# Two decoder layers on one core: the opening's split moved ahead, the gate's modulation as PE bursts, rotary embedding in two operations, and the first layer's masks as PE products

## The chip, the core and the metric

The kernel runs on one core of one Trainium2 chip. The time is device microseconds of one execution on that core, and the median of the runs is compared. Engines: PE (TensorE, with PEld for its weight loads), DVE (VectorE), ACT (ScalarE), POOL (GpSimd); SP issues nearly all transfers.

## What is computed

Two layers (D = 1024, 256 tokens, one sequence, all float32). Each layer is a token mixer and a gated feed-forward part, both between norms whose scale, shift and gate come from a conditioning vector `c`. Cut to what the change touches:

```python
c_act = silu(c)
for l in range(2):
    sh_m, sc_m, gt_m, sh_f, sc_f, gt_f = split(c_act @ w_ada[l] + b_ada[l], 6)
    h = rms_norm(x, g_pre_mix[l]) * (1 + sc_m) + sh_m
    x = x + gt_m * rms_norm(token_mixer(h, ...), g_post_mix[l])
    h = rms_norm(x, g_pre_ffn[l]) * (1 + sc_f) + sh_f
    x = x + gt_f * rms_norm(conv_glu_ffn(h, ...), g_post_ffn[l])
# token_mixer: proj = h @ w_in -> mq mk mv dq dk dv (8 heads of 64 each), qi (8 heads), ki, wi
# rotary embedding on the first 16 of 64 dims of mq, mk, dq, dk, qi, ki
# mq mk mv: causal softmax attention (256 tokens are one block)
# indexer: score[t,s] = sum_h wi[t,h] relu(qi[t,h] . ki[s]); the 64 best admissible keys are kept
# dq dk dv: softmax attention over the kept keys; group norms; @ w_out
```

## The kernel before, in words

**Products in split precision.** A float32 weight tile is split into a high part (`wh`, made by ACT, L139) and a low part (`wl`, made by the DVE, L140); so are the activations (`hh`, `hl`). A product is three matmuls: hh.wh, hh.wl, hl.wh. All weights come in one stream in the order of use, by `load` (L108), into six rotating buffers of 1 MB (`raw`) that SP fills in order. A buffer is free when its split, or the reduction that reads it, is done.

**The opening** (`start`, L576) computes the first four chunks of the first layer's projection (ia, ib, mq, mk) while it computes the modulation of its input. It goes over eight blocks k of 128 features. For each, `modulation_v` (two reductions of 128x1024 on the DVE, L653) or, for k = 0, 3 and 6, `modulation` (eight matmuls of 32 columns by 256, L664, on the PE) gives shift and scale; `modulate` (L637) then splits the first 584 weight columns (`divide(k, 0)`), makes hh and f with two ACT operations (L644, L646), hl on the DVE (L647), and splits the other 1,024 columns (`divide(k, 1)`). `products` (L689) issues the 24 matmuls of a block. Everything here is pinned to the order of the program; block k + 1's modulation is written into the middle of block k's products.

**The mixer.** The PE's main line is `project` (L357) for mv, dq, dk, dv and then the output projection (`out_row`, 96 matmuls). Beside it run background chains (`Background`, L42): a chain is a generator that yields how many ticks it waits; the main line gives one tick for each k of a projection. Chains carry the gate and the feed-forward modulation (`gemv_v`, L182, one 128x1024 reduction a column on the DVE), the transposes of heads, the indexer (L393), the two attentions (`attend`, L427) and the group norms. `burst` (L384) issues a group of matmuls back to back. Between what is pinned a scheduler orders each engine's instructions by priority and by its own model of readiness.

**Scores and masks.** `scores` in `attend` computes a set of four heads by 128 keys, or two by 256, into banks 4 and 5, then one DVE operation a head (L449) adds the mask and takes the maximum into SBUF, ACT exponentiates that copy (L453), the DVE normalises (L461) and the PE transposes (L468). The masks are float32, 0 or -1e30: `lateneg` for the causal group, the indexer's two DVE operations (L423, L424) for the other.

**Embedding.** `rope_out` (L329) evacuates on ACT and applies the embedding with three DVE operations (L338 to L340). `ki_T` copies the transposed index key with the DVE (L757).

**The boundary** (L310) adds the gated, normed mixer output to x (`residual`, L290), normalises again, transposes and modulates; it needs the feed-forward scale and shift, so `bg.drain("sf")` stands before it (L859). The feed-forward part is 22 steps of `up` and `down`.

## Time and profile before

| | |
|---|---|
| median of 3 runs | 696.31 us (695.06 to 696.6) |
| the profiled execution | 694.81 us |
| its span in the trace | 693.0 us, mean granted clock 0.994 |
| PE / DVE / ACT busy | 662.4 / 560.6 / 422.4 us |
| moved by DMA | 163.02 MB, mean 235 GB/s |

The profile is of one execution; its span is from the first to the last instruction, and the execution's own time is 1.8 us longer. A matmul's end in the profile is modelled, so the distance from one start to the next tells more than its length. Busy time in a stretch of the trace is read against that stretch, not against the whole program: the stages have different limits.

### The profile page before, as it was taken

What the parts mean: (1) busy time and instruction counts of PE and PEld (TensorE: products, weight loads), DVE (VectorE), ACT (ScalarE), POOL (GpSimd) and SP (SyncE); (2) the same over time, 40 slices, a digit from 0 to 9 for tenths busy, and PEclk for the clock granted to TensorE, in tenths of its full rate; (3) what the DMA queues carried; (4) which work ended last, traced back from release to release, by engine and by line L of the source; (5) the groups of instructions that cost most, each with busy time, mean ns of one, the idle gap of its engine ahead of it and who ended that gap; (6) DMA issues with size and microseconds to landing.
All of it is one profiled execution on the core that took longest, in us unless ns stands there. A gap on an engine that the chain in (4) does not pass through costs nothing.

```text
span 693.0 us, 11206 instructions
## 1 busy us (share of the span) xinstructions
PE 662.4 (96%) x4257; PEld 569.1 (82%) x4257; DVE 560.6 (81%) x1130; ACT 422.4 (61%) x781; POOL 31.8 (5%) x56
## 2 busy tenths in 40 slices
PE   7999988997999999999999998999999999999996
PEld 4777766775899999999988776877789999999994
DVE  5779999999799999988669996678679886666553
ACT  5446567994865555555565657879586555555441
POOL 1000001012000000000020000000100000000000
PEclk9999999999999999999999999999999999999998
DMA  8997963766479999998444933345336895555001
GB/s 363 419 363 269 404 244 130 295 216 249 155 288 360 375 375 335 338 337 316 167 171 177 348 124 122 122 155 200 132 150 228 302 341 187 220 183 183 1 1 61
DMA packets 24517, 163.02 MB, mean 235 GB/s; under 512 B 3312, under 2 KB 3728, under 8 KB 6160
## 3 DMA queue, kind: packets, MB, share of 16 engines
q1 hardware_dynamic: 23184, 159.77, 61.2%
q0 software_dynamic: 704, 2.11, 1.0%
q8 instruction: 33, 0.54, 0.3%
q10 hardware_dynamic: 576, 0.43, 0.2%
q14 instruction: 20, 0.16, 0.1%
HBM read 161.24 MB, written 1.06 MB: 234 GB/s over the span
## 4 chain that ended last, share of the span: by engine, by line
PE 67%; DVE 18%; ACT 9%; issue 4%; POOL 1%; DMA 1%; SPq 0%; POOLq 0%; DVEq 0%; ACTq 0%
PE b L540 18%; PE b L539 18%; PE b L541 18%; PE b L369 7%; DVE raw L189 4%; DVE wl L140 3%; ACT t L453 2%; DVE iscore L420 2%; PE b L695 2%; DVE iscore L412 2%; DVE tiny L419 1%; PE b L389 1%; ACT wh L135 1%; ACT t L232 1%; PE b L468 1%
## 5 line engine op out<-in xcount | busy, mean ns | idle before, releaser
L140 DVE TENSOR_TENSOR wl<-raw,wh 128x1024 fp32r<-128x1024 f32 (+1 forms) x146 | 173.6, 1195 | 34.7 <-ACT wh L139 30.9
L539 PE MATMUL b<-hh,wh 128*128 128x256 f32 x640 | 180.0, 281 | 0.0
L541 PE MATMUL b<-hl,wh 128*128 128x256 f32 x640 | 179.7, 281 | 0.0
L540 PE MATMUL b<-hh,wl 128*128 128x256 f32 x640 | 179.7, 281 | 0.0
L139 ACT ACTIVATE wh<-raw 128x1024 fp32r<-128x1024 f32 (+1 forms) x146 | 149.2, 1045 | 45.2 <-PE b L541 36.4
L540 PEld LDWEIGHTS b<-hh,wl 128*128 128x128 f32 x640 | 122.5, 191 | 1.4
L539 PEld LDWEIGHTS b<-hh,wh 128*128 128x128 f32 x640 | 120.3, 188 | 1.4
L541 PEld LDWEIGHTS b<-hl,wh 128*128 128x128 f32 x640 | 120.1, 188 | 0.0
L189 DVE SCALAR_TENSOR_TENSOR raw<-raw,crow 128x1024 f32<-128x1024 f32 x80 | 96.2, 1219 | 1.4 <-DMA raw<-in_stream_dram 1.4
L369 PE MATMUL b<-wh,hh 128*128 128x512 f32 (+1 forms) x184 | 72.7, 397 | 0.0
L369 PE MATMUL b<-wh,hl 128*128 128x512 f32 (+1 forms) x184 | 68.5, 386 | 0.0
L139 ACT ACTIVATE dh<-raw 128x1024 fp32r<-128x1024 f32 (+2 forms) x47 | 49.7, 1059 | 25.8 <-PE b L540 25.8
L140 DVE TENSOR_TENSOR dl<-raw,dh 128x1024 fp32r<-128x1024 f32 (+2 forms) x47 | 56.8, 1210 | 8.9 <-ACT dh L139 8.9
L912 ACT ACTIVATE t<-b,smt 128x256 f32<-128x256 f32 x44 | 25.1, 571 | 57.4 <-PE b L541 57.3
L539 PE MATMUL b<-dh,t 128*128 128x512 f32 x152 | 59.7, 393 | 0.0
L540 PE MATMUL b<-dh,t 128*128 128x512 f32 x152 | 59.6, 392 | 0.0
L541 PE MATMUL b<-dl,t 128*128 128x512 f32 x152 | 59.2, 389 | 0.0
L369 PE MATMUL b<-wl,hh 128*128 128x512 f32 (+1 forms) x184 | 55.2, 391 | 2.7 <-DVE wl L140 2.7
L369 PEld LDWEIGHTS b<-wl,hh 128*128 128x128 f32 x184 | 33.9, 189 | 10.8 <-DVE wl L140 4.0
L369 PEld LDWEIGHTS b<-wh,hh 128*128 128x128 f32 x184 | 34.6, 188 | 7.3 <-issue 1.0
L369 PEld LDWEIGHTS b<-wh,hl 128*128 128x128 f32 x184 | 33.8, 188 | 5.9
L913 DVE SCALAR_TENSOR_TENSOR t<-b,smt,t 128x255 f32<-128x255 f32 x44 | 21.1, 480 | 20.7 <-ACT t L912 20.6
(167 smaller groups left out, 1105.2 us busy)
## 6 DMA issues: line engine op xcount, KB each, us to landing
raw<-in_stream_dram SPq DMA_DIRECT2D x143, 1024.0 KB, 6.5
raw<-in_stream_dram SPq DMA_DIRECT2D x8, 804.0 KB, 8.2
gate<-gated POOLq DMA_DIRECT2D x4, 512.0 KB, 7.0
xt<-in_x_dram SPq DMA_DIRECT2D x2, 512.0 KB, 4.1
raw<-in_stream_dram SPq DMA_DIRECT2D x1, 984.0 KB, 5.9
out_dram<-xt SPq DMA_DIRECT2D x2, 256.0 KB, 2.1
raw<-in_stream_dram SPq DMA_DIRECT2D x1, 328.0 KB, 5.0
out_dram<-xt ACTq DMA_DIRECT2D x1, 256.0 KB, 2.1
```

What stands on the lines that cost most here:

```text
L139: put(nc.scalar.activation(out=hi[:, :n], in_=raw, func=AF.Copy))
L140: put(nc.vector.tensor_tensor(out=lo[:, :n], in0=raw, in1=hi[:, :n].bitcast(F32), op=OP.subtract))
L189: nc.vector.scalar_tensor_tensor(out=ri, in0=ri, scalar=1.0, in1=crow, op0=OP.mult, op1=OP.mult, accum_out=mods[l][:, j + i:j + i + 1])
L369: mm = lambda l_, k, i, start=False, stop=False: nc.tensor.matmul(a[:, :n], lhsT=l_[:, k, tt], rhs=w[k][i], start=start, stop=stop)
L412: nc.vector.scalar_tensor_tensor(out=sc, in0=r[:, j * nk:j * nk + nk], scalar=wi[:, h:h + 1], in1=fill[:, 256 - nk:] if first else sc, op0 ...
L420: nc.vector.match_replace(out=sc, in_to_replace=m8, in_values=sc, imm_value=MARK)
L453: nc.scalar.activation(out=ev[:, j, :], in_=ev[:, j, :], func=AF.Exp, bias=nm[:, j:j + 1], scale=-1.0, accum_out=sm[:, j:j + 1])
L539: nc.tensor.matmul(y, lhsT=hh, rhs=wh, start=first, stop=False)
L540: nc.tensor.matmul(y, lhsT=hl, rhs=wh, start=False, stop=False)
L541: nc.tensor.matmul(y, lhsT=hh, rhs=wl, start=False, stop=last)
L912: nc.scalar.activation(out=z, in_=p[:, :256], func=AF.Identity, scale=w2[:, i:i + 1], bias=bc[:, i:i + 1])
L913: nc.vector.scalar_tensor_tensor(out=z[:, 1:], in0=p[:, :255], scalar=w1[:, i:i + 1], in1=z[:, 1:], op0=OP.mult, op1=OP.add)
```

## The change

Four parts. All lines below 192 are unchanged, so L139, L140 and L189 keep their numbers; later ones move by 22 and more.

1. In the opening `divide(k, 1)` comes before the two modulating ACT operations for k > 0.
2. The first layer's gate columns (16 to 24) go from eight DVE reductions to `gemv_p`: two rounds of two loads, a burst of 16 matmuls, an ACT copy, four transposes and one small DVE sum. The feed-forward shift columns (24 to 32) take the place of the gate in the early chain, with 6 ticks between, and only 32 to 40 are left to the later one.
3. `rope_out` multiplies by cosine and sine in one DVE operation over 16 columns twice, and adds the swapped half in a second; `ki_T` copies with ACT. Both layers.
4. In the first layer masks are bf16 zeros and ones. A product with `negi` (-1e30 times the identity) puts them into the score banks ahead of the scores, in the same burst; the DVE takes one maximum a bank, and ACT exponentiates from the bank.

```diff
+    def gemv_p(l, j0, j1, wait, gap):
+        yield wait
+        for j in range(j0, j1, 4):
+            r = [load(("p", l, j + 2 * i, 2048))[0] for i in range(2)]
+            yield gap
+            p = tp_bank()
+            burst([(p[32 * (i % 4):32 * (i % 4) + 32, 256 * h:256 * h + 256], cs32[:, i, :],
+                    r[h][:, 256 * i:256 * i + 256], dict(start=i < 4, stop=i >= 4, skip_group_check=True))
+                   for h in range(2) for i in range(8)])
+            e = t2()
+            nc.scalar.activation(out=e, in_=p, func=AF.Copy)
+            yield 4
+            q = tp_bank()
+            for b in range(4):
+                nc.tensor.transpose(q[:, 128 * b:128 * b + 128], e[:, 128 * b:128 * b + 128], ident)
+            nc.vector.tensor_reduce(out=mods[l][:, j:j + 4], axis=AX.X, op=OP.add,
+                                    in_=q.rearrange("p (b g r) -> p b g r", b=4, g=4)[:, :, :, 0])
+            yield 1
...
@@ rope_out
-        nc.vector.tensor_tensor(out=n[:, :, 0], in0=x, in1=cosv, op=OP.mult)
-        nc.vector.tensor_tensor(out=n[:, :, 1].rearrange("p h (a b) -> p h a b", a=2), in0=y, in1=sinv, op=OP.mult)
-        nc.vector.tensor_tensor(out=x, in0=n[:, :, 0], in1=n[:, :, 1], op=OP.add)
+        nc.vector.tensor_tensor(out=n, in0=x[:, :, None, :].to_broadcast([128, nh, 2, 16]),
+                                in1=rt[:, t][:, None].to_broadcast([128, nh, 2, 16]), op=OP.mult)
...
+        nc.vector.tensor_tensor(out=halves(x), in0=halves(n[:, :, 0]), in1=y, op=OP.add)
@@ indexer
+        if pe:
+            nc.vector.scalar_tensor_tensor(out=mask, in0=sc, scalar=-2.0e38, in1=late[:, 256 - nk:],
+                                           op0=OP.is_gt, op1=OP.max)
@@ attend, scores
+            left = masks[t] if masks is not None else lateb if pe else lateneg[:, 256 - nk:]
+            flags = dict(start=not pe, stop=True, skip_group_check=pe)
+            burst([(pv[:, :, nk - left.shape[-1]:], negi, left[:, None, :].to_broadcast([128, nh, left.shape[-1]]),
+                    dict(start=True, stop=False, skip_group_check=True)) for pv in (pp[::-1] if pe else ())]
+                  + [(pp[par][:, j, :], qT[64 * par:64 * par + 64, b * nh + j, 128 * t:128 * t + 128],
+                      kT[64 * par:64 * par + 64, b * nh + j, :nk], flags)
+                     for j in range(nh) for par in (1, 0)])
...
+                if pe:
+                    nc.vector.tensor_reduce(out=nm, in_=pv, axis=AX.X, op=OP.max, negate=True)
-                    nc.scalar.activation(out=ev[:, j, :], in_=ev[:, j, :], func=AF.Exp, bias=nm[:, j:j + 1],
-                                         scale=-1.0, accum_out=sm[:, j:j + 1])
+                    nc.scalar.activation(out=ev[:, j, :], in_=(pv if pe else ev)[:, j, :], func=AF.Exp,
+                                         bias=nm[:, j:j + 1], scale=1.0 if pe else -1.0,
+                                         accum_out=sm[:, j:j + 1])
@@ modulate, in the opening
             divide(k, 0)
+            if k:
+                divide(k, 1)
             xk = xT[k // 4][:, k % 4, :]
...
-            divide(k, 1)
+            if k == 0:
+                divide(k, 1)
@@ ki_T
-            nc.vector.tensor_copy(kiT[:, 128 * t:128 * t + 128], p[:, :128])
+            nc.scalar.copy(kiT[:, 128 * t:128 * t + 128], p[:, :128])
@@ the layers
-            bg.add("gt", gemv_v(l, 16, 24, 6))
+            bg.add("sf", gemv_v(l, 24, 32, 6))
+            bg.add("gt", gemv_p(l, 16, 24, 34, 16))
...
-            bg.add("sf", gemv_v(l, 24, 40, 9))
+            bg.add("sf", gemv_v(l, 32, 40, 9))
```

The order on the engines at three places, as the two programs have it. First the DVE in the opening, for k = 2: before, hl stands between the two low halves.

```order
L653 SCALAR_TENSOR_TENSOR raw,mod_99<-raw,crow 128x1024 x2
L639 SCALAR_TENSOR_TENSOR prescale<-mod_99,plus_161,smt 128x1
L641 TENSOR_TENSOR mod_99<-mod_99,smt 128x1
L140 TENSOR_TENSOR wl<-raw,wh 128x584
L647 TENSOR_TENSOR hl<-t_290,hh 128x256
L140 TENSOR_TENSOR wl<-raw,wh 128x1024
```

And in the changed program:

```order
L689 SCALAR_TENSOR_TENSOR raw,mod_99<-raw,crow 128x1024 x2
L672 SCALAR_TENSOR_TENSOR prescale<-mod_99,plus_161,smt 128x1
L674 TENSOR_TENSOR mod_99<-mod_99,smt 128x1
L140 TENSOR_TENSOR wl<-raw,wh 128x584
L140 TENSOR_TENSOR wl<-raw,wh 128x1024
L682 TENSOR_TENSOR hl<-t_294,hh 128x256
```

hl (L647, now L682) moved behind the wide low half; ACT's wide `wh` moved ahead of its two modulations in the same way.

Second, ACT at the end of the opening, before: the two splits of mv's first load come before the evacuations of ia (b_215, b_218), ib (b_214), mq (b_216, b_219) and mk (b_217, b_220).

```order
L139 ACTIVATE wh<-raw 128x1024 x3
L331 ACTIVATE t_592<-b_215 128x256
...
L331 ACTIVATE t_607<-b_214 128x256
L331 ACTIVATE t_635<-b_216 128x512
L331 ACTIVATE t_641<-b_219 128x512
L331 ACTIVATE t_647<-b_217 128x512
L331 ACTIVATE t_653<-b_220 128x512
L139 ACTIVATE wh<-raw 128x1024 x2
```

In the changed program:

```order
L353 ACTIVATE t_592<-b_215 128x256
...
L353 ACTIVATE t_605<-b_214 128x256
L139 ACTIVATE wh<-raw 128x1024 x2
L353 ACTIVATE t_629<-b_216 128x512
L353 ACTIVATE t_634<-b_219 128x512
L353 ACTIVATE t_639<-b_217 128x512
L353 ACTIVATE t_644<-b_220 128x512
L139 ACTIVATE wh<-raw 128x1024 x2
```

The four wide evacuations now stand between the first and the second pair of mv's splits.

Third, the DVE at the boundary, before: L189 are the reductions for scale and shift, L296 the residual's products, L304 its sums, L264 the normalising.

```order
L532 TENSOR_TENSOR o<-o,b_1623 128x512
L189 SCALAR_TENSOR_TENSOR raw,mod_99<-raw,crow 128x1024
L534 TENSOR_TENSOR hl<-o,hh 128x4x128
L189 SCALAR_TENSOR_TENSOR raw,mod_99<-raw,crow 128x1024 x3
L296 TENSOR_TENSOR t_1749<-b_1463,gate 128x512
L192 TENSOR_TENSOR mod_99<-mod_99,smt 128x16
L296 TENSOR_TENSOR t_1750<-b_1464,gate 128x512
L198 SCALAR_TENSOR_TENSOR prescale<-mod_99,smt 128x8
L304 SCALAR_TENSOR_TENSOR xt<-t_1749,tiny_1759,xt 128x512
L304 SCALAR_TENSOR_TENSOR xt<-t_1750,tiny_1759,xt 128x512
L296 TENSOR_TENSOR t_1773<-b_1465,gate 128x512
L264 TENSOR_SCALAR t_1778<-xt,tiny_1770 128x512
```

In the changed program, where these lines are L318, L326 and L286:

```order
L318 TENSOR_TENSOR t_1768<-b_1494,gate 128x512
L565 TENSOR_TENSOR o<-o,b_1654 128x512
L567 TENSOR_TENSOR hl<-o,hh 128x4x128
L318 TENSOR_TENSOR t_1769<-b_1495,gate 128x512
L326 SCALAR_TENSOR_TENSOR xt<-t_1768,tiny_1778,xt 128x512
L326 SCALAR_TENSOR_TENSOR xt<-t_1769,tiny_1778,xt 128x512
L189 SCALAR_TENSOR_TENSOR raw,mod_99<-raw,crow 128x1024
L140 TENSOR_TENSOR wl<-raw,wh 128x1024
L318 TENSOR_TENSOR t_1792<-b_1496,gate 128x512
L286 TENSOR_SCALAR t_1797<-xt,tiny_1789 128x512
```

No reduction stands ahead of the residual's first products any more; one, and a split, now stand between the sums and the normalising.

## Rows read from the trace of the kernel before

**Rows 1.** The page, part 1: busy time of each engine, its share of the span, and instructions.

```profile
PE 662.4 (96%) x4257; PEld 569.1 (82%) x4257; DVE 560.6 (81%) x1130; ACT 422.4 (61%) x781; POOL 31.8 (5%) x56
```

**Rows 2.** The table by stretches: start and end, its length, then for each engine busy us and instructions, the granted TensorE clock (1.00 is 2.4 GHz), the share of the DMA engines' time, GB/s. In order: the opening's eight blocks, the first layer's mixer up to its last output product, the boundary, the first layer's feed-forward part, the second layer's mixer.

```profile
12.30:57.80 45.50, 41.97 (x229) 32.08 (x230) 34.47 (x66) 25.55 (x46) 0.00 (x0) 1.00 0.99 390
57.80:163.40 105.60, 98.50 (x588) 75.32 (x586) 103.55 (x293) 75.72 (x165) 11.46 (x8) 1.00 0.69 261
163.40:176.40 13.00, 8.44 (x38) 6.54 (x38) 9.99 (x21) 7.95 (x23) 3.12 (x6) 0.87 0.44 163
181.00:350.00 169.00, 169.00 (x1209) 158.88 (x1208) 153.90 (x235) 94.85 (x138) 1.16 (x2) 1.00 0.84 315
365.00:480.00 115.00, 111.86 (x666) 88.65 (x664) 96.06 (x268) 82.08 (x179) 2.81 (x5) 1.00 0.47 171
```

**Rows 3.** The DVE's timeline in the opening (start us, duration us, engine, line, operation, tiles, and in brackets the idle time before it with what ended it): one period for k = 2, from the reductions of one block (L653) to those of the next.

```profile
14.89 1.22 DVE L653 SCALAR_TENSOR_TENSOR raw<-raw,crow 128x1024 f32<-128x1024 f32 x1
...
18.75 0.42 DVE L647 TENSOR_TENSOR hl<-t,hh 128x256 fp32r<-128x256 f32 x1 [0.49 <-ACT t L646]
19.70 1.23 DVE L140 TENSOR_TENSOR wl<-raw,wh 128x1024 fp32r<-128x1024 f32 x1 [0.53 <-ACT wh L139]
20.84 1.22 DVE L653 SCALAR_TENSOR_TENSOR raw<-raw,crow 128x1024 f32<-128x1024 f32 x1
```

**Rows 4.** ACT's timeline at the end of the opening, in the same columns: six evacuations in a row, two of 256 columns and four of 512.

```profile
56.48 2.63 ACT L331 ACTIVATE t<-b 128x256 f32<-128x256 f32 x6
```

**Rows 5.** The PE's timeline in the opening, in the same columns. L695 are a block's products, whose first has 328 columns; L664 is a modulation on the PE; L369 is the first projection of the mixer.

```profile
18.28 0.42 PE L695 MATMUL b<-wh,hh 128*128 128x328 f32 x1
...
19.72 0.50 PE L695 MATMUL b<-wh,hh 128*128 128x512 f32 x1
20.98 0.50 PE L695 MATMUL b<-wl,hh 128*128 128x512 f32 x1 [0.76 <-DVE wl L140]
21.32 0.40 PE L695 MATMUL b<-wh,hh 128*128 128x512 f32 x1
21.56 0.39 PE L695 MATMUL b<-wl,hh 128*128 128x512 f32 x1
...
24.23 0.42 PE L695 MATMUL b<-wh,hh 128*128 128x328 f32 x1
...
25.50 1.07 PE L664 MATMUL b<-raw,cs 128*32 128x256 f32 x16
...
30.34 0.31 PE L695 MATMUL b<-wh,hh 128*128 128x328 f32 x1
...
57.77 0.39 PE L369 MATMUL b<-wh,hh 128*128 128x512 f32 x1
```

**Rows 6.** Groups by line in the first layer's mixer, first the DVE's, then one of ACT's (line, engine, operation, tiles, shapes, count | busy us, mean ns of one | idle before).

```profile
L189 DVE SCALAR_TENSOR_TENSOR raw<-raw,crow 128x1024 f32<-128x1024 f32 x24 | 28.8, 1220 | 0.0
L449 DVE CUSTOM_DVE_ANT_0 t<-b,lateneg 128x128 f32<-128x128 f32 (+1 forms) x16 | 5.2, 345 | 0.0
L449 DVE CUSTOM_DVE_ANT_0 t<-b,mask 128x128 f32<-128x128 f32 (+1 forms) x16 | 4.9, 351 | 0.0
L461 DVE TENSOR_TENSOR t<-t,rs 128x512 f32<-128x512 f32 x6 | 4.1, 684 | 0.0
L449 DVE DVE_READ_ACCUMULATOR2_ANT tiny<- 128x1 f32 x32 | 2.6, 82 | 0.0
L453 ACT ACTIVATE t<-t,tiny 128x128 f32<-128x128 f32 x16 | 6.2, 388 | 0.0
```

**Rows 7.** What the PE's matmuls waited for in the first layer's mixer (engine, line, releaser: us in total, times, longest).

```profile
PE b L369 <- DVE wl L140: 2.7, 3, 1.6
PE b L346 <- DVE t L340: 1.4, 2, 0.9
PE b L389 <- DVE tiny L449: 1.4, 2, 1.2
PE b L528 <- POOL tiny L525: 0.8, 1, 0.8
PE b L468 <- DVE t L461: 0.6, 1, 0.6
```

**Rows 8.** The boundary, first the DVE's timeline, then the PE's: L189 are the last reductions for scale and shift, L296 the residual's products, L304 the residual sums, L264 the normalising; L541 is the last output product, L252 the transposes of the normalised rows.

```profile
158.08 1.22 DVE L189 SCALAR_TENSOR_TENSOR raw<-raw,crow 128x1024 f32<-128x1024 f32 x1
...
161.51 0.69 DVE L296 TENSOR_TENSOR t<-b,gate 128x512 f32<-128x512 f32 x1
...
162.87 1.41 DVE L304 SCALAR_TENSOR_TENSOR xt<-t,tiny,xt 128x512 f32<-128x512 f32 x2
...
166.25 0.89 DVE L264 TENSOR_SCALAR t<-xt,tiny 128x512 f32<-128x512 f32 x2
...
163.14 0.40 PE L541 MATMUL b<-wl,hh 128*128 128x512 f32 x1
166.80 1.97 PE L252 MATMUL b<-ident,t 128*128 128x128 f32 x8 [3.26 <-DVE t L264]
```

**Rows 9.** Prices: eight transposes and three products of 512 bf16 columns on the PE in the first microseconds (timeline), and loads of 1,024 KB in the mixer, with the median time from issue to landing in us.

```profile
6.20 0.81 PE L562 MATMUL b<-late,negi 128*128 128x512 bf16 x3
...
10.50 1.04 PE L615 MATMUL b<-ident,t 128*128 128x128 f32 x8
...
raw<-in_stream_dram SPq DMA_DIRECT2D x12, 1024.0 KB, 7.6
```

More of the change, by code (lines that the diff above doesn't have):

```diff
@@ L391, in burst, with indexer @@
                 pin(ins)
-    def indexer(t, qiT, kiT, wi, res):
+    def indexer(t, qiT, kiT, wi, res, pe):
         nk = 128 * (t + 1)
@@ L446, in scores @@
                 ev = e.rearrange("p (h k) -> p h k", h=nh)
-                for j in range(nh):
-                    nc.vector.tensor_tensor_reduce(out=ev[:, j, :], in0=pv[:, j, :], in1=mask, scale=-1.0,
+                if pe:
+                    nc.vector.tensor_reduce(out=nm, in_=pv, axis=AX.X, op=OP.max, negate=True)
+                for j in range(0 if pe else nh):
+                    nc.vector.tensor_tensor_reduce(out=ev[:, j, :], in0=pv[:, j, :], in1=left, scale=-1.0,
                                                    scalar=-FILL, op0=OP.add, op1=OP.min, accum_out=nm[:, j:j + 1])
@@ L805, in trunk @@
         for t in range(2):
-            bg.add("att", indexer(t, qiT, kiT, wis[t], masks))
+            bg.add("att", indexer(t, qiT, kiT, wis[t], masks, l == 0))
         tps["free"] = [6]
```

29 lines of the change are left out of this document (15 added, 14 removed).

## The prediction

> **What bounds the kernel now.** I read the page's busy line first: the PE is busy for 662.4 of 693.0 us and the DVE for 560.6 [rows 1]. A mean over the program says little about four edits that nearly all lie in the first 180 us, so the table by stage came next [rows 2]. The reader is to see four stages there. In the opening (12.3 to 57.8) the PE idles 3.5 us, while DVE and ACT are far from full. In the first layer's mixer (57.8 to 163.4) the DVE is busy 103.55 of 105.6 us, and the PE idles 7.1 us. In the 13 us at the boundary to the feed-forward part the PE idles 4.6 us, and its granted clock falls to 0.87 of the full 2.4 GHz. From 181 to 350 the PE is busy all 169.00 us: nothing that this change does to DVE or ACT can shorten that, and I cost it at nothing as long as the PE is its cover. The second layer's mixer is like the first one and sees two small edits alone.
>
> Then the opening by instruction. It is eight blocks of products, one for each k. A block with its modulation on the DVE lasts 18.28 to 24.23, 5.95 us, one with the next modulation on the PE 24.23 to 30.34, 6.11 us; the last block ends at 57.77 [rows 5]. In the first of these, the product at 20.98 starts 1.26 us after the one before, where its likes follow at 0.24 us: it waits 1.0 us for the DVE's low half of the 1,024-column split. The DVE's period is 5.95 us as well (14.89 to 20.84), with two waits in it: 0.49 us for ACT's second modulation, then 0.53 us for ACT's copy of those 1,024 columns [rows 3]. ACT makes that copy behind its two modulations, though it needs nothing from them. So DVE and ACT take turns, and the PE pays. For the mixer I read the PE's waits: of 6.9 us, 6.1 end at a DVE instruction, 0.8 at POOL [rows 7].
>
> **The change, part by part.**
>
> Opening. From k = 1 on ACT splits the 1,024 columns before the modulations, while the DVE is still at its two reductions, and the DVE's low half moves ahead of hl. Both DVE waits should go: 5.95 - 0.49 - 0.53 = 4.9 us for its period [rows 3]. The PE's block without its wait is 5.95 - 1.0 - 0.4 (slow starts behind waits) = 4.5 us [rows 5]. Block 0 keeps its old order. Block 1, which the DVE still leads, comes to 4.9 us, blocks 3, 4, 6 and 7 to the PE's 4.5, blocks 2 and 5, which carry a modulation on the PE, to 6.0: together 4.9 + 4 x 4.5 + 2 x 6.0 = 34.9, against 57.77 - 18.28 = 39.5 now [rows 5]. The gain is 4.6; I take **-4.6 us**, with 4.0 and 5.3 as ends.
>
> Gate's modulation. Eight reductions leave the DVE: 8 x 1.22 = 9.8 us of its busy time [rows 6]. The PE gets two bursts of 16 matmuls; eight of that form took 1.07 us [rows 5], so 4.1, and eight transposes; eight took 1.04 with the tail [rows 9], so 0.9. ACT's two copies and the DVE's two small sums lie beside other work.
>
> Masks. Twelve products of -1e30 times the mask: 5,120 columns in all; three of 512 took 0.81 us [rows 9], so 2.3 to 2.7. With the turns between narrow and wide forms the PE's additions come to **+7.5 us** (6.5 to 8). All of it lies on the PE, so it hides only in PE idle time. The DVE's 32 masked copies and their 32 accumulator reads cost 5.2 + 4.9 + 2.6 = 12.7 us; instead come 12 maxima over 512 columns. Nothing in the trace is such a maximum; the nearest row is the 128x512 product at 684 ns [rows 6], so 8.2, and 4.5 us less.
>
> Embedding in two operations and the two kiT copies on ACT: some 1 us less DVE in each mixer. In the first that is in the sum; in the second I take **-0.5 us** (0 to -1.1), since its PE idles 3.1 us of 115 and only part of that can be the DVE's [rows 2].
>
> Mixer, together. The DVE loses 9.8 + 4.5 + 1 = 15 of 103.55 us, and the PE becomes the bound. Waits for the DVE's wl (2.7), its embedding (1.4) and its normalising (0.6) I take as gone: **-4.7 us** (-2.4 to -6.1) [rows 7]. The 1.4 us in which a score burst waited for the masked copies to free its banks I keep: the banks are now freed by ACT's exponentials, that read them, instead. POOL's 0.8 stays. New is a wait at the start: four evacuations of 512 columns now stand between the two pairs of splits of the first projection. They are 2.0 of the 2.63 us that ACT took for six [rows 4], the third split 1.0 more; the PE has eight products at 0.24 and four transposes, 2.4, so it waits **+0.6 us**.
>
> Boundary. Now three reductions stand on the DVE between 158.08 and 161.51, ahead of the residual's first product, which had been ready; the chain behind them ends with the normalising at 166.25, and the PE, done at 163.14 + 0.23, idles to 166.80 [rows 8]. The reductions for scale and shift start earlier now, where the gate's had been, and none is left there: 3.4 us. But a reduction and a split of 1.14 each have slipped in ahead of the normalising, between 162.87 and 166.25, into a gap of 1.4 us in which the DVE waited for ACT's squares; that gives 0.9 back. The eight transposes took 1.97 us at the lower clock, against 1.04 at the full one; with 0.9 us idle instead of 3.4 I expect the full one: 0.7. **-3.2 us** (-2 to -4).
>
> Sum: -4.6 + 7.5 - 4.7 + 0.6 - 3.2 - 0.5 = **-4.9 us**. The profiled execution took 694.81, so 689.9; the median of the runs shown is 696.31, 1.5 above it, and by that the forecast is **691.4 us**. What a measurement of this kernel can tell from no change is about 0.2%, 1.4 us.
>
> **One rule against this sum.** In the mixer the PE's weight loads are busy 75.32 of 105.6 us, its matmuls 98.50 [rows 2]. The Trainium skill (Perfetto Trace Analysis, Identifying the Most-Contended Engine) says that matmul busy time is a poor measure of what is left on TensorE, and that the share of weight loads and the achieved flops are the ones to use. By that 30 us would be free, the additions would cost nothing, and the sum would be -12.4. The trace speaks against it here: the 512-column products follow each other at 0.24 us with no wait between them [rows 5], so a PE that only streams cannot take more of them. It stands as the first rival.
>
> **The rivals.**
> 1. The PE has room: the additions fit between products. For it: the loads' 71%, where the feed-forward stage shows 158.88 of 169 [rows 2]. Against it: the 0.24 us. 691.4 - 7.5 = 683.9. Chance 0.06.
> 2. Score bursts wait for ACT. Each burst that follows another needs both banks, so the second half's exponentials too, four of 388 ns, 1.5 us, in the first token tile [rows 6], two of the wider ones, some 1.0, in the second. Four such places make 5.0 us, where I kept 1.4: 691.4 + 3.6 = 695.0. For it: the same place already waits 1.4 [rows 7]. Against: wide products stand between most bursts. Chance 0.11.
> 3. The opening does not shorten, because transfers pace it: the DMA share is 0.99 [rows 2]. Against: 45.5 us at 390 GB/s are 17.7 MB, and eight blocks of 1,024 + 804 KB are 15.0; the rest runs ahead. 691.4 + 4.6 = 696.0. Chance 0.08.
> 4. Slower: each of the gate's two bursts holds two of the six weight buffers until the PE has run it, where a DVE reduction freed them before. SP's queue is in order, so a later load waits for the burst. Such a load lands 7.6 us after its issue [rows 9], and its split takes 1.0 more. If it carries projection weights and the PE reaches their products sooner than 8.6 us after the burst, the PE waits for the rest; at half of that for each of two bursts it is 8.6 us, 700.0. Against: none of the PE's waits there ends at a transfer now [rows 7]. Chance 0.09.
>
> **How the numbers follow.** My forecast has 0.66. Rivals 1 and about half of 2 end faster by over 0.2%: 0.66 + 0.06 + 0.05 = 0.77. The other half of 2 and 3 are within it: 0.14. Rival 4 is slower: 0.09. The range takes the better ends of the terms (-5.3 + 6.5 - 6.1 - 4 - 1.1 = -10.0, so 686.3 by the median) and, above, rivals 2 and 3 with the worse ends: 686 to 697.5. It leaves out rivals 1 and 4, 0.15.
>
> **What would show it.** Block 1 ends near 23.0 and the opening near 53.0; no wait of PE for wl in it from k = 1 on. In the mixer DVE busy falls to about 88 us of a stage nearly as long as before, and the PE's idle time to 3 us. The residual's products start right behind the last output products of the first token tile, and the granted clock at the boundary stays at 1.00. I am wrong if the opening ends after 56, if PE waits for a transfer or for ACT's exponentials by more than 3 us in the mixer, or if its DVE stays above 98 us.

## The result

The changed kernel takes **691.23 us**, median of five runs (691.12 to 692.67), the kernel before 695.06 in the five runs beside it. The ratio is 0.9946, 95% interval 0.9931 to 0.9962: 3.8 us faster, with 2.6 to 4.8 as ends. The forecast was 691.4, with 686.0 to 697.5 as its range. The number hit better than its sum did: the sum said -4.9, and it was put on a median of 696.31, where the four later sets of runs of the kernel before, 9 to 23 each, have medians of 694.9 to 695.1. From 695.0 the forecast would have been 690.1. The sum was 1.1 us too good and its base 1.3 us too slow; that these cancel is luck.

Both kernels' times come in two groups about 1.4 us apart (691.1 to 691.2 and 692.4 to 692.7 here; 694.5 to 695.4 and 695.6 to 696.9 before). The profiled execution of before, 694.81, lies in its lower group, that of after, 692.67, in its upper one. So the spans, 693.0 and 690.9, differ by 2.1 us only; where the rest went is shown below.

Where the time went, by the start of the same product in both timelines (us):

| product on the PE | before | after | difference so far |
|---|---|---|---|
| first of the mixer's projection | 57.77 | 52.72 | -5.05 |
| last output product of the first mixer | 163.14 | 161.63 | -1.51 |
| first of the feed-forward part | 183.32 | 177.54 | -5.78 |
| a down product 9 us later | 192.28 | 188.40 | -3.88 |
| second layer's mixer, its first score burst | 415.84 | 411.13 | -4.71 |
| same mixer, a transpose near its end | 478.38 | 476.43 | -1.95 |

**Whole program and stages.** The page's first part, and the table by stretches (columns as in [rows 2]) for the opening, the first mixer, the boundary, most of the feed-forward part and the second mixer.

```profile
PE 668.3 (97%) x4341; PEld 573.1 (83%) x4341; DVE 550.2 (80%) x1031; ACT 423.7 (61%) x787; POOL 26.1 (4%) x56
```

```profile
12.30:52.70 40.40, 39.24 (x228) 32.21 (x229) 33.45 (x74) 25.35 (x45) 0.00 (x0) 1.00 1.02 418
52.70:161.90 109.20, 106.09 (x672) 78.87 (x670) 97.77 (x208) 78.68 (x177) 6.50 (x10) 1.00 0.70 261
161.90:170.90 9.00, 7.52 (x39) 5.61 (x39) 7.36 (x17) 6.31 (x18) 2.40 (x4) 1.00 0.58 224
175.00:346.00 171.00, 169.44 (x1210) 159.13 (x1209) 154.21 (x235) 95.02 (x138) 1.16 (x2) 1.00 0.84 311
361.00:476.00 115.00, 111.36 (x655) 88.13 (x654) 92.98 (x250) 80.50 (x176) 2.81 (x5) 0.99 0.47 170
```

Against [rows 2] the mixer's PE busy time rose from 98.50 to 106.09 and its idle time fell from 7.1 to 3.1; the boundary's clock went from 0.87 to 1.00; and the feed-forward part, whose PE was busy without a break, now has 1.56 us of idle time in it.

**Opening.** The DVE's timeline, one period for k = 2 as in [rows 3], then the PE's: the first products of blocks 1 and 2, and the mixer's first product, as in [rows 5].

```profile
14.86 1.22 DVE L689 SCALAR_TENSOR_TENSOR raw<-raw,crow 128x1024 f32<-128x1024 f32 x1
...
17.47 1.90 DVE L140 TENSOR_TENSOR wl<-raw,wh 128x584 fp32r<-128x584 f32 x2
19.29 0.42 DVE L682 TENSOR_TENSOR hl<-t,hh 128x256 fp32r<-128x256 f32 x1
19.62 1.22 DVE L689 SCALAR_TENSOR_TENSOR raw<-raw,crow 128x1024 f32<-128x1024 f32 x1
```

```profile
18.25 0.42 PE L731 MATMUL b<-wh,hh 128*128 128x328 f32 x1
...
23.00 0.42 PE L731 MATMUL b<-wh,hh 128*128 128x328 f32 x1
...
52.72 0.39 PE L391 MATMUL b<-wh,hh 128*128 128x512 f32 x1
```

Both waits of the DVE are gone (no bracket is left), and its period is 19.62 - 14.86 = 4.76 us instead of 5.95. Block 1 lasts 4.75.

**First mixer.** What the PE waited for (as in [rows 7]), and two of the DVE's groups (as in [rows 6]).

```profile
PE b L501 <- DVE t L494: 1.2, 2, 0.6
PE b L391 <- DVE wl L140: 0.6, 2, 0.4
PE b L368 <- DVE t L362: 0.5, 2, 0.4
PE b L391 <- ACT wh L139: 0.3, 1, 0.3
```

```profile
L189 DVE SCALAR_TENSOR_TENSOR raw<-raw,crow 128x1024 f32<-128x1024 f32 x17 | 20.3, 1217 | 0.0
...
L478 DVE TENSOR_REDUCE tiny<-b 128x2 f32<-128x512 f32 (+1 forms) x12 | 8.2, 681 | 0.0
```

**Boundary.** The DVE's timeline and the PE's, as in [rows 8]: L318 is the residual's product, L286 the normalising, L574 the last output product, L274 the transposes.

```profile
160.59 0.68 DVE L318 TENSOR_TENSOR t<-b,gate 128x512 f32<-128x512 f32 x1
161.43 0.88 DVE L286 TENSOR_SCALAR t<-xt,tiny 128x512 f32<-128x512 f32 x2 [0.16 <-POOL tiny L264]
162.23 1.22 DVE L189 SCALAR_TENSOR_TENSOR raw<-raw,crow 128x1024 f32<-128x1024 f32 x1
```

```profile
161.63 0.39 PE L574 MATMUL b<-wl,hh 128*128 128x512 f32 x1
161.97 1.09 PE L274 MATMUL b<-ident,t 128*128 128x128 f32 x8
```

The transposes follow the last product at once, where 3.26 us lay between, and take 1.09 instead of 1.97 us.

**Start of the feed-forward part.** The PE's timeline, then the DVE's: L950 and L952 are the two DVE operations of the first convolution, which free the bank that the PE wants next; L140 are splits.

```profile
183.43 0.28 PE L574 MATMUL b<-hl,wh 128*128 128x256 f32 x1
185.26 0.36 PE L572 MATMUL b<-hh,wh 128*128 128x256 f32 x1 [1.56 <-DVE t L952]
```

```profile
181.93 1.22 DVE L140 TENSOR_TENSOR wl<-raw,wh 128x1024 fp32r<-128x1024 f32 x1
183.07 0.48 DVE L950 SCALAR_TENSOR_TENSOR t<-b,smt,t 128x255 f32<-128x255 f32 x1
183.50 1.22 DVE L140 TENSOR_TENSOR wl<-raw,wh 128x1024 fp32r<-128x1024 f32 x1
184.64 0.48 DVE L952 SCALAR_TENSOR_TENSOR t<-b,smt,t 128x254 f32<-128x254 f32 x1
```

Ahead of each of the two operations stands a split of 1.2 us on the DVE's in-order queue, and the PE waits for the second one. In the kernel before the two stood side by side, as L913 and L915, and no matmul waited there:

```profile
187.92 0.48 DVE L913 SCALAR_TENSOR_TENSOR t<-b,smt,t 128x255 f32<-128x255 f32 x1
188.43 0.48 DVE L915 SCALAR_TENSOR_TENSOR t<-b,smt,t 128x254 f32<-128x254 f32 x1
```

**Second layer.** The PE's timeline where the profiled execution loses 1.6 us more: the second score burst, its transposes, four products of 512 columns. Then the stretch around them, for its clock.

```profile
417.83 1.13 PE L411 MATMUL b<-kT,qT 64*128 64x256 f32 x8 [1.42 <-DVE tiny L481]
419.87 1.01 PE L501 MATMUL b<-ident,t 128*128 128x128 f32 x4 [0.91 <-DVE rs L489]
420.53 2.05 PE L391 MATMUL b<-wl,hh 128*128 128x512 f32 x4
```

```profile
419.00:424.00 5.00, 4.13 (x16) 3.54 (x16) 2.85 (x11) 1.29 (x5) 0.00 (x0) 0.66 0.05 21
```

After two waits, 1.42 and 0.91 us with 1.1 us of work between them, the granted clock is 0.66 over the stretch, and four products take 2.05 us; the same four take 1.17 at the full clock (profile of the kernel with the convolution's order, below). From the second score burst to the third it is 8.42 us here and 6.82 us there.

### The profile page after: what moved, and what is told of

The parts are those of the page before. It is cut to its first block, busy times and chain, and to the rows that moved or that the text cites. A ratio compares the mean times of both kernels' runs of the same rounds, so it can differ in the third digit from the quotient of the medians.

```text
span 690.9 us, 11286 instructions
## 1 busy us (share of the span) xinstructions
PE 668.3 (97%) x4341; PEld 573.1 (83%) x4341; DVE 550.2 (80%) x1031; ACT 423.7 (61%) x787; POOL 26.1 (4%) x56
## 4 chain that ended last, share of the span: by engine, by line
PE 75%; DVE 11%; ACT 7%; issue 4%; DMA 1%; POOL 1%; SPq 0%; POOLq 0%; DVEq 0%; ACTq 0%
PE b L572 18%; PE b L573 18%; PE b L574 18%; PE b L391 12%; PE b L731 3%; DVE wl L140 3%; PE b L411 3%; PE b L501 1%; DVE iscore L442 1%; DVE tiny L441 1%; DVE iscore L434 1%; ACT t L485 1%; DVE raw L689 1%; PE b L368 1%; DMA raw<-in_stream_dram 1%
## 5 line engine op out<-in xcount | busy, mean ns | idle before, releaser
L140 DVE TENSOR_TENSOR wl<-raw,wh 128x1024 fp32r<-128x1024 f32 (+1 forms) x146 | 173.2, 1196 | 33.3 <-ACT wh L139 28.9
L139 ACT ACTIVATE wh<-raw 128x1024 fp32r<-128x1024 f32 (+1 forms) x146 | 149.5, 1047 | 52.0 <-PE b L574 41.3
L574 PE MATMUL b<-hl,wh 128*128 128x256 f32 x640 | 179.6, 281 | 0.0
L574 PEld LDWEIGHTS b<-hl,wh 128*128 128x128 f32 x640 | 120.1, 188 | 0.0
L189 DVE SCALAR_TENSOR_TENSOR raw<-raw,crow 128x1024 f32<-128x1024 f32 x72 | 86.7, 1219 | 0.7 <-DMA raw<-in_stream_dram 0.7
L140 DVE TENSOR_TENSOR dl<-raw,dh 128x1024 fp32r<-128x1024 f32 (+2 forms) x47 | 56.8, 1211 | 9.4 <-ACT dh L139 9.3
L139 ACT ACTIVATE dh<-raw 128x1024 fp32r<-128x1024 f32 (+2 forms) x47 | 49.7, 1059 | 23.0 <-PE b L573 23.0
L574 PE MATMUL b<-dl,t 128*128 128x512 f32 x152 | 59.2, 389 | 0.0
L950 DVE SCALAR_TENSOR_TENSOR t<-b,smt,t 128x255 f32<-128x255 f32 x44 | 21.2, 481 | 23.1 <-ACT t L949 23.0
```

What stands on the lines that cost most here:

```text
L139: put(nc.scalar.activation(out=hi[:, :n], in_=raw, func=AF.Copy))
L140: put(nc.vector.tensor_tensor(out=lo[:, :n], in0=raw, in1=hi[:, :n].bitcast(F32), op=OP.subtract))
L189: nc.vector.scalar_tensor_tensor(out=ri, in0=ri, scalar=1.0, in1=crow, op0=OP.mult, op1=OP.mult, accum_out=mods[l][:, j + i:j + i + 1])
L574: nc.tensor.matmul(y, lhsT=hh, rhs=wl, start=False, stop=last)
L950: nc.vector.scalar_tensor_tensor(out=z[:, 1:], in0=p[:, :255], scalar=w1[:, i:i + 1], in1=z[:, 1:], op0=OP.mult, op1=OP.add)
```

## The experiments

Each is one kernel, timed in 5 to 12 executions beside the kernel before on the same chip. The first ones take the change apart.

**Opening alone** (the kernel before with the opening's edit):

```diff
             divide(k, 0)
+            if k:
+                divide(k, 1)
...
-            divide(k, 1)
+            if k == 0:
+                divide(k, 1)
```

> The kernel before with the opening's edit alone (from k = 1 on both splits ahead of the modulation); nothing else changed. Theory A, the gain of the opening is kept to the end, since the first layer's mixer begins 5.05 us earlier in the changed kernel (52.72 instead of 57.77) and nothing behind it hangs on a clock of its own: about 5 us under the kernel before, 690.0. Theory B, the mixer is bound by the DVE and by its loads, which do not come earlier, so that the PE meets them 5 us sooner and waits: only 2 to 3 us are left, 692 to 693.

Measured: 694.81 against 694.93, ratio 0.9995 [0.9986, 1.0004]. **No gain**, worse than theory B. Its mixer does begin 5.0 us earlier, and 4 of them are gone at its end. The stretch of the mixer, three stretches in it for the clock, and the PE's longest waits:

```profile
52.70:162.00 109.30, 102.46 (x587) 76.74 (x587) 104.64 (x281) 77.79 (x168) 9.49 (x8) 0.97 0.71 264
102.00:104.00 2.00, 1.02 (x5) 0.71 (x4) 2.00 (x10) 1.52 (x2) 0.00 (x0) 0.57 0.06 25
104.00:106.00 2.00, 1.43 (x7) 0.82 (x6) 2.00 (x9) 0.74 (x2) 0.00 (x0) 0.50 0.00 0
106.00:108.00 2.00, 2.00 (x14) 1.67 (x16) 2.00 (x11) 1.41 (x4) 0.00 (x0) 0.50 0.00 0
```

```profile
PE b L468 <- DVE t L461: 1.9, 3, 1.0
PE b L389 <- DVE tiny L449: 1.7, 1, 1.7
```

The DVE has the same work as before (104.64 us, [rows 2] shows 103.55) and is busy nearly throughout. The PE, five microseconds sooner at the same bursts, waits for it, and behind these waits its granted clock falls to the lower level, 1.2 GHz, from about 102 to 109 us. The boundary gives 1.6 us back (from the last output product to the first of the feed-forward part it takes 18.59 us, before 20.18), and 1.8 are lost again at the first convolution (a wait of 1.6 us, as in the changed kernel). The profiled execution, 694.02, one of the faster ones of this kernel, keeps 0.8.

**Everything but the opening** (the changed kernel with the opening's two lines back in their old places):

> The changed kernel with the opening in its old order; gate, place of the reductions, masks and embedding as changed. With the kernel before (695.0), the opening alone (694.8) and the whole change (691.2) it completes a square. Theory A, opening and the rest each help only together: the rest puts 3.5 us more than it saves into the mixer and takes 2.4 from the boundary, so without the opening it is 695 to 696.5, no gain at all. Theory B, the rest brings the whole gain and the opening none, as the opening alone suggests: 691 to 692.

Measured: 695.59 against 695.05, ratio 1.0007 [0.9998, 1.0016]. Theory A holds. Its mixer is as long as that of the changed kernel, 109.2 us, with 3.9 idle on the PE:

```profile
57.80:167.00 109.20, 105.34 (x672) 78.52 (x670) 97.92 (x216) 78.11 (x176) 6.51 (x9) 1.00 0.68 256
```

So the square is: neither 695.0, opening alone 694.8, the rest alone 695.6, both 691.2. One half gives nothing, the other nothing or a loss of half a microsecond, and together they give 3.8. Where the halves meet is read from the four profiles, by the start of the same products (us):

| kernel | mixer starts | its length, to the last output product | from there to the feed-forward part | from there to the same down product |
|---|---|---|---|---|
| before | 57.77 | 105.37 | 20.18 | 8.96 |
| opening alone | 52.76 | 109.36 | 18.59 | 10.79 |
| the rest alone | 57.76 | 108.66 | 17.37 | 8.96 |
| both | 52.72 | 108.91 | 15.91 | 10.86 |

Three columns add up: the start of the mixer comes from the opening alone, the boundary's -1.6 and -2.8 make -4.3, the start of the feed-forward part's +1.8 and 0 make +1.9. The mixer's do not: it is 4.0 us longer with the opening alone, 3.3 with the rest alone, and with both 3.5 and not 7.3. With the rest alone and with both the PE has 6.7 and 7.5 us more to do, waits 3.4 and 4.0 us less, and keeps the full clock. With the opening alone it waits no longer in sum than before (idle 6.8 us, before 7.1), but the same products take it 102.5 us instead of 98.3; the granted clock of 0.72 over the 12 us from 100 on makes 3.4 us of that, by my estimate. Whether the PE, at the full clock, would have waited for the DVE instead was not tested. I read it so: the gain of the opening passes through the first mixer only if the DVE is relieved there (its last output product comes 4.8 us earlier than with the rest alone); and the relief, which puts work on the PE, costs there as much as the boundary gives back, unless the PE comes early.

**Gate back on the DVE** (and all sixteen reductions for scale and shift at their old place):

```diff
-            bg.add("sf", gemv_v(l, 24, 32, 6))
-            bg.add("gt", gemv_p(l, 16, 24, 34, 16))
+            bg.add("gt", gemv_v(l, 16, 24, 6))
...
-            bg.add("sf", gemv_v(l, 32, 40, 9))
+            bg.add("sf", gemv_v(l, 24, 40, 9))
```

> The changed kernel with the gate's modulation back on the DVE and the reductions for the feed-forward scale and shift back in their old place; opening, masks, embedding as changed. Theory A, by my sum: the PE loses 2 x 1.93 us of bursts and 2 x 0.6 of transposes, the DVE gets 8 x 1.15 = 9.2 us back in a stage where it is busy 97.77 of 109.2, so that it binds again (107.0 of 104.2, +2.8), and the boundary's gain of 2.4 net (-4.3, then +1.9 at the start of the feed-forward part) goes: about 691.3, no difference. Theory B, the gate's edit is a loss by itself (the PE pays 5 us, the DVE had room): 688 or less. Theory C, it carries the change: 694 or more.

Measured: 692.01 (690.37 to 692.29), ratio 0.9949 [0.9937, 0.9961]. As theory A says, no difference that can be told in the median, though four of its five runs lie in the upper group; the fifth, the profiled one, is 0.75 under the lowest run of the changed kernel. The boundary's gain does not go, as theory A had it: the PE waits 0.25 us there, though the reductions are back at their old place in the program.

```profile
163.18 1.09 PE L274 MATMUL b<-ident,t 128*128 128x128 f32 x8 [0.25 <-DVE t L286]
```

**Masks back on the DVE** (the last argument of `indexer` and `attend` False in both layers):

> The changed kernel with the masks of the first layer added on the DVE again, as before; opening, gate and embedding as changed. Theory A: the PE loses the twelve products (2.3 to 2.7 us), and the DVE, 90 per cent busy in the stage, takes the copies back without holding the PE up by as much; the waits of score bursts for the copies come back (1.4 us in the trace of before): 690 to 691. Theory B, as in my sum, the masks' 4.5 us of DVE time are part of what freed the PE of its waits: these come back by 3 us or more, less 2.5: 692 or more.

Measured: 691.05 (690.87 to 692.42), ratio 0.9944 [0.9933, 0.9956]. Theory A. The first mixer in these two kernels, gate on the DVE first:

```profile
52.70:162.00 109.30, 102.09 (x597) 75.35 (x596) 102.56 (x218) 78.38 (x175) 6.71 (x9) 1.00 0.73 270
```

```profile
52.70:162.00 109.30, 104.41 (x659) 77.61 (x659) 98.89 (x260) 79.79 (x176) 5.89 (x8) 1.00 0.71 264
```

With the masks back the DVE is busy 98.89 us, against 97.77 without them: 1.1 us more, where my sum said 4.5. With the gate back it is 4.8 us more, though eight reductions of 1.15 us, 9.2, are back in the stretch. Busy time in an equal stretch is not the work of the stage: a DVE that is free sooner takes work of the next stage into it (in the changed kernel both normalisings of the boundary, with the gate back none).

**Neither gate nor masks** (opening and embedding only, both of the edits above at once):

> The kernel before with the opening's edit and the embedding's (two operations instead of three, and the two copies of kiT on ACT), the gate and the masks as before. The opening alone gave nothing, 694.8, with the masks or with the gate added to both edits the time was 692.0 and 691.05. Theory A, the opening's gain is held up by the DVE, which had 104.6 us to do in 109.3 there, and the embedding's some 2 us are too little to let it through: 693.5 to 695. Theory B, it was the embedding that let it through, the masks and the gate cost and give the same: 691 to 692.

Measured: 695.98 (694.21 to 699.41, twelve runs), ratio 1.0011 [0.9998, 1.0024]. Nearer to theory A, and worse than it: no gain. In the profiled execution (694.66, one of the fastest) the DVE is busy 103.47 of 109.3. Of the opening's 5.0 us 3.2 are gone at the last output product, at 161.36, with a granted clock of 0.98 in the stretch; but that is no later than in the changed kernel. The rest goes behind it. A reduction waits 1.69 us for its transfer ahead of the normalising, the PE waits 3.60 us, its transposes take 1.60, and the first convolution costs 1.6 more:

```profile
163.06 1.23 DVE L189 SCALAR_TENSOR_TENSOR raw<-raw,crow 128x1024 f32<-128x1024 f32 x1 [1.69 <-DMA raw<-in_stream_dram]
```

```profile
165.35 1.60 PE L274 MATMUL b<-ident,t 128*128 128x128 f32 x8 [3.60 <-DVE t L286]
```

With either of the two reliefs alone (gate back, masks back) the time is that of the changed kernel; the second adds nothing that can be measured. The longest execution of this kernel, 699.41, has the lowest mean granted clock, 0.984, against 0.992 and 0.994 in the two shortest; no long one was profiled.

**Reductions late** (gate on the PE, all reductions for scale and shift at their old place):

```diff
-            bg.add("sf", gemv_v(l, 24, 32, 6))
...
-            bg.add("sf", gemv_v(l, 32, 40, 9))
+            bg.add("sf", gemv_v(l, 24, 40, 9))
```

> The changed kernel with the gate on the PE, and the first eight of the sixteen reductions for the feed-forward scale and shift put back behind the attention's start, where all sixteen stood before. It tells apart what made the boundary shorter. Theory A, their place did: the last reductions stand ahead of the residual's products again, and the boundary takes 2 to 4 us longer: 693 to 695. Theory B, the eight reductions that left the DVE altogether did, and the place is worth nothing: 691.

Measured: 694.74, ratio 0.9998 [0.9989, 1.0007]. Theory A: with the gate on the PE, where the reductions stand is worth 3.5 us. The DVE's timeline at its boundary, then the PE's:

```profile
163.04 1.23 DVE L189 SCALAR_TENSOR_TENSOR raw<-raw,crow 128x1024 f32<-128x1024 f32 x1 [1.15 <-DMA raw<-in_stream_dram]
```

```profile
165.33 1.89 PE L274 MATMUL b<-ident,t 128*128 128x128 f32 x8 [2.83 <-DVE t L286]
```

A reduction waits 1.15 us for its transfer, the normalising stands behind it on the same queue, and the PE waits 2.83 us and then runs its eight transposes at 1.89 us, the lower clock.

This run has both reliefs and gains nothing, and the kernel with the gate back has the reductions at the same old place and gains. What they differ in is the order that came out on the DVE. From the profiles of six kernels, all with the early opening:

| kernel | last output product | reductions in the 5 us ahead of the residual's first product | PE's wait at the transposes | first of the feed-forward part |
|---|---|---|---|---|
| opening alone | 162.12 | 3 | 2.63 | 180.71 |
| neither gate nor masks | 161.36 | 3 | 3.60 | 180.90 |
| reductions late | 162.10 | 2 | 2.83 | 180.93 |
| masks back | 162.03 | 0 | 1.42 | 178.87 |
| gate back | 162.53 | 0 | 0.25 | 178.53 |
| whole change | 161.63 | 0 | 0.1 | 177.54 |

The mixer ends within 1.2 us in all six, though the PE's work in it differs by up to 7.5. Where reductions are left over ahead of the residual, one more waits for its transfer ahead of the normalising (0.43, 1.69 and 1.15 us), the feed-forward part starts some 2 us later or more, and the kernel gains nothing. Why they come early enough with the gate on the DVE and too late with it on the PE, from the same place in the program, was not tested.

**Gate's bursts twice** (each burst of 16 products run two times into the same bank):

```diff
+            for _ in range(2):
             burst([(p[32 * (i % 4)...
```

> The changed kernel with each of the gate's two bursts of products run twice in a row into the same bank; nothing else differs. It measures the price of PE work added to the mixer. Theory A, the PE binds there (3.1 us idle in 109.2): the second runs cost about what they take, 2 x 1.9 = 3.8 us less at most 1 us of waits that they fill, 694 to 695. Theory B, the PE has room between products: 691.2. Theory C, it starts a chain of waits at the DVE or of a lower clock: over 696.

Measured: 694.15 (693.39 to 695.66), ratio 0.9989 [0.998, 0.9997]. Its mixer and boundary end 4.0 us later than in the changed kernel: theory A at that place. Of these, 1.9 come back at once, because there is no wait at the first convolution, so the whole kernel pays 2.3 (lowest run) to 2.9 (median).

**The first convolution's order:**

```diff
             if i > 2:
-                st["behind"] = ()
+                st["behind"] = (convs[0],) if i == 3 else ()
...
-            nc.vector.scalar_tensor_tensor(out=z[:, 2:], in0=p[:, :254], ...
+            conv = nc.vector.scalar_tensor_tensor(out=z[:, 2:], in0=p[:, :254], ...
...
+            convs.append(conv.ins)
```

> The changed kernel with two splits of the feed-forward part held behind the first convolution's second operation, so that on the DVE the two operations of the first convolution stand side by side again, as in the kernel before; in the changed kernel a split stood ahead of each. Theory A, the PE's wait of 1.6 us at 183.7 in the changed kernel comes from this order alone: 1.6 to 1.9 us faster, 689.5. Theory B, the DVE and ACT are behind by as much after the shorter boundary, and the wait goes to the next split or convolution: 691.

Measured: 691.03 (690.56 to 691.82), ratio 0.9943 [0.993, 0.9956]; the lowest run is 0.6 under the lowest of the changed kernel. Between the theories: the wait is gone, 1.5 us are gained there, and half of it is lost in the next 12 us, in steps of some 0.3 us without a wait that the profile names; the DVE is busy 14.16 of 14.50 us there. The DVE's timeline, with the two operations side by side:

```profile
182.65 0.48 DVE L952 SCALAR_TENSOR_TENSOR t<-b,smt,t 128x255 f32<-128x255 f32 x1 [0.52 <-ACT t L951]
183.17 0.48 DVE L954 SCALAR_TENSOR_TENSOR t<-b,smt,t 128x254 f32<-128x254 f32 x1
```

**Products into the wait of the second layer.** First four, on the changed kernel:

```diff
         def scores(i):
             t, b = sets[i]
+            if i == 1 and masks is None and not pe:
+                keep_warm(4)
```

> The changed kernel with four products that nobody reads (128x512, bf16) ahead of the second score burst of the first attention in the second layer, where the PE waited 1.42 and 0.91 us for the DVE and then ran at half its clock from 419.9 to 423. They fall into idle time. Theory A, the two groups of times of every kernel here (691.1 to 691.2 and 692.4 to 692.7 for the changed one, 694.9 and 696.3 for the kernel before) differ by this fall of the clock: with the products nearly all executions are in the lower group, 691.2, and none at 692.5. Theory B, the clock at this place is not what divides the groups: as before, both groups, 2 of 5 above 692.

Measured: 693.18 (691.91 to 693.5), ratio 0.9966 [0.9954, 0.9978]. A miss: both groups stayed, and the lowest run rose by 0.8. The four took the place of as many projection products, which went behind the burst, and the wait was 1.46 us, as long as before. So ten, on the kernel with the convolution's order:

> The kernel with the splits held behind the first convolution (median 691.03), with ten products that nobody reads (128x512, bf16) ahead of the second score burst of the second layer; four of them only pushed three projection products behind the burst, and the PE waited as long as before. Ten take 2.3 us and cover the wait of 1.4. Theory A, the two groups of times differ by the clock behind this wait: all executions within 0.6 us of each other and none 1.3 above, at 690.6 to 691.5, since the ten displace some products. Theory B, the groups have another cause: both groups as before.

Measured: 691.39, all five runs between 691.26 and 691.63, ratio 0.9941 [0.9929, 0.9953]. As theory A says, no run lies in an upper group; where two runs in five do, five in the lower would come out by chance 8 times in 100. The ten displaced five projection products behind the burst, so that from the second burst to the third it is 8.32 us at the full clock. The PE's timeline, and the stretch with its clock:

```profile
414.25 2.33 PE L597 MATMUL b<-late,negi 128*128 128x512 bf16 x10
416.96 1.13 PE L411 MATMUL b<-kT,qT 64*128 64x256 f32 x8 [0.38 <-DVE tiny L483]
419.00 0.63 PE L503 MATMUL b<-ident,t 128*128 128x128 f32 x4 [0.91 <-DVE rs L491]
```

```profile
416.00:424.00 8.00, 6.52 (x46) 4.53 (x45) 5.27 (x25) 6.42 (x25) 0.00 (x0) 1.00 0.29 119
```

**Half a gate** (one burst, four reductions more, on the kernel with the convolution's order):

> The kernel with the splits held behind the first convolution, with half of the gate's modulation on the PE and half on the DVE (one burst instead of two, four reductions more). Theory A, PE and DVE are near balance in the mixer (3.1 us idle on the PE, 11 on the DVE), so that a half burst less, 2.5 us, is mostly gained as long as 4 x 1.15 = 4.6 us find room on the DVE: 689 to 690. Theory B, whatever moves from one to the other is given back by waits, as with the gate or the masks taken back whole: 690.6 to 692.

Measured: 692.75 (691.52 to 692.78), ratio 0.9957 [0.9944, 0.997]. Theory B: the PE has 102.84 us to do in 109.3, the DVE 100.31, and the PE waits for both DVE and ACT.

**Embedding of the second layer as before** (three operations, its kiT copies on the DVE; on the kernel with the convolution's order):

> The kernel with the splits held behind the first convolution (median 691.03, lower group 690.6), with the embedding of the second layer in three operations again and its two kiT copies on the DVE again, as in the kernel before; the first layer keeps both edits. It tests the second layer's term of my sum, 0.5 us to the good. Theory A, as in the sum: 0.5 to 1 us slower, 691.5 or more. Theory B, by the traces, in which kernels with the edit lose 0.4 us between 375 and 480 against the kernel before and wait 1.42 and 0.91 us for the DVE at the second score burst instead of 1.1 and 0.5: 0.4 us faster, 690.2 to 690.6, and the waits go back to 1.1 and 0.5.

Measured: **689.82**, all five runs between 689.74 and 690.1, ratio 0.9921 [0.9908, 0.9935]: faster than both kernels, by 1.2 us than the one it is made from; the two profiled executions differ by 0.8, 0.4 of it in the second mixer. Theory B, by more than its number. The waits in the second layer:

```profile
PE b L427 <- DVE tiny L497: 1.1, 1, 1.1
PE b L517 <- DVE rs L505: 0.5, 1, 0.5
```

They are those of the kernel before, and its timeline keeps a distance of 4.84 us from that of before through the whole second mixer:

```profile
PE b L389 <- DVE tiny L449: 1.1, 1, 1.1
PE b L468 <- DVE rs L456: 0.5, 1, 0.5
```

The operations and the kiT copies were put back together; which of the two it is was not tested.

## Why the prediction was right, and where it was wrong

By terms, from the two profiles:

| term | forecast | measured |
|---|---|---|
| opening | -4.6 | -5.05 |
| PE's additions in the mixer | +7.5 | +7.6 (busy 98.50 to 106.09) |
| PE's waits there, with the new one | -4.1 | -4.0 (idle 7.1 to 3.1) |
| boundary | -3.2 | -4.3 |
| start of the feed-forward part | 0 | +1.9 |
| second layer | -0.5 | +0.4 (mask kernel's profile); +2.0 with the fall of the clock |

- **Opening.** Block by block as worked out: block 1 ends at 23.00, the mixer begins at 52.72. But the term counted as if it stood for itself. It doesn't: alone it gives nothing, because the mixer is then 4.0 us longer. The sum held because it cost the mixer for the whole change, as +7.5 - 4.1 = +3.4 where +3.5 was measured.
- **PE's additions.** Right, and work added to the changed kernel is paid in full there: the run with both bursts doubled, 3.8 us of work, moved the start of the feed-forward part back by 4.0. Rival 1 is out. By the rule that stood against the sum (the Trainium skill, Perfetto Trace Analysis, Identifying the Most-Contended Engine) the weight loads' 78.87 of 109.20 us leave room; the run that tests it, the doubled bursts, found none.
- **PE's waits.** The total is right, its parts are not: of the waits taken as gone (wl 2.7, embedding 1.4, normalising 0.6) 2.3 us are left, the normalising's doubled to 1.2, and those taken as kept (score bursts for the DVE 1.4, POOL 0.8) are gone. That the two make up for each other is luck.
- **The DVE's relief.** Wrong in size: I had 88 us left in the mixer, it is 97.77, and the sign of being wrong that I gave, above 98, was missed by 0.2 only. The masks' term failed: 12.7 us were sums of the means of instructions that overlap, with their accumulator reads counted in full (in the profile of before a copy follows the last at 0.21 us, or at 0.34 for 256 columns). Taken off the DVE they free 1.1. What I left out is work of the next stage that moves into the stretch: two more splits, one reduction, one product and one sum of the residual and both normalisings, some 6 us by their means. The maxima are as estimated, 681 ns against the 684 of the nearest row. It did no harm: with the masks back the kernel takes 691.05. The sum did not see that either.
- **Score bursts.** Rival 2 has 0.2 us of wait for ACT in a burst. Out.
- **Opening paced by transfers.** Rival 3 is out: the same loads ran at 418 instead of 390 GB/s.
- **Weight buffers.** Rival 4 in its stated form is out, no matmul of the changed kernel waits for a transfer in the mixer. A relative of it is real: with the reductions late, the boundary waited for one's transfer.
- **Boundary.** Mis-sized to the safe side: I gave 0.9 us back for a reduction and a split that slip in ahead of the normalising, and the PE waits 0.1. The clock stayed at 1.00 as forecast. What carried it is that no reduction is left over ahead of the residual; with the gate on the PE that takes the new place of the reductions, with the gate on the DVE it did not.
- **The step that failed** is "I cost it at nothing as long as the PE is its cover", on the feed-forward part. The PE comes there 5.8 us earlier, the order on the DVE is another one, a split ahead of each of the first convolution's operations, and one wait of 1.6 us opens. With the order put back the wait is gone. It is not the earlier start by itself: with the gate or the masks back the part starts 4.8 or 4.5 us earlier than before and no matmul waits there.
- **Second layer.** Of the wrong sign. The embedding's own waits fall by 0.5 us (1.0 to 0.5), but one of the products that stood behind the second score burst now stands ahead of it (17 instead of 16 between the two bursts), and the two waits at the burst grow by 0.7 us in all. With the embedding and the kiT copies undone, 1.2 us came back in the median.

Open: where the clock falls in the upper group of the kernel before, with waits of 1.1 and 0.5 us at this burst, when the last kernel has the same waits and one group; no profile of its upper group was taken. That it falls somewhere is on record: in the 72 later executions of the kernel before, the mean granted clock is 0.9945 in the 50 below 695.5 us and 0.9920 in the 22 above. By my estimate a group gap of 1.4 us at half the clock is 0.002 of the mean. That the fall divides the groups of the changed kernel and of those made from it rests on the run with ten products and on six profiles: the three with a fall there (692.67, 693.18 with four products, 692.78 with half a gate) lie in the upper groups of their kernels, the three without (690.37 with the gate back, 690.91 with the masks back, 690.63 with the convolution's order) in the lower ones. The 1.6 us that the stretch takes longer with the fall are about the gap between the groups. The changed kernel itself has one profile, in its upper group.

## What to carry to other kernels

Where two engines are near balance in a stage, a gain ahead of it and a relief in it can be worth nothing one by one, as here, where both gave 3.8 us; cost them together, and say which engine ends the stage in each case. Then look behind the stage: what it leaves over on an in-order queue decides when the next one starts. When a stage comes earlier, read the order of the in-order queues at the start of the next one, even if its bound has no gap. Busy time in a stretch can hold work of the next stage. Sums of mean durations overstate short instructions that overlap; take the distance from start to start.

## What the runs showed of the hardware

- Idle time of the PE cost more than itself: behind waits of 1.72, 0.98 and 0.47 us within 6 us (opening alone) the granted clock went to 0.57, 0.50 and 0.50 in three stretches of 2 us, though products stood between the waits. In the kernel before, waits of 1.19, 0.63 and 0.56 us at the same bursts, within 5 us, left it at 1.00.
- The same waits, 1.42 and 0.91 us, were followed by a fall of the clock in the profile of the changed kernel (0.66 over 5 us) and by none in that of the convolution's order (1.00 over 8 us). The two groups of the changed kernel's times lie 1.2 to 1.5 us apart.
- A DVE maximum over 128x512 out of a bank takes 681 ns, about as long as a product of two such tiles (684 in [rows 6]).
